# Rounds of the state-space layer in another order, states exchanged by GpSimd, an output product kept whole

## The chip, the cores and the metric

The kernel runs on one core of a Trainium2 chip. The metric is the device time of one execution in microseconds; a kernel is run several times and the median counts. TensorE (PE) multiplies matrices out of SBUF into PSUM, VectorE (DVE) and ScalarE (ACT) work element by element, GpSimd (POOL) does that too and issues transfers, SyncE (SP) only issues transfers. Each engine executes its own queue; they wait for one another through semaphores.

## The reference

A two-layer decoder trunk for one sequence of 1024 tokens and width 1024, all in float32. Layer 0 is a block-diagonal state-space mixer: the normed and modulated input is projected to u and z; u is cut into 64 groups of 16 channels, each with 64 complex states.

```python
u, z = jnp.split(h @ w_in, 2, axis=-1)
bu = einsum('blgc,gpc->blgp', u, bb)            # complex: real and imaginary part
s[l] = abar * s[l-1] + bu[l]                    # associative scan over the tokens
y = einsum(s_r, C_re) - einsum(s_i, C_im) + D * u
y = gelu(y)
y = y * sigmoid(y @ w_glu + b_glu) * silu(z)
x = x + gate * (y @ w_out)
```

Then keys, values and forget gates are computed once from x, and layer 1 is attention with 16 heads whose scores are shifted by the summed forget gates, gated by silu(z) and projected. Every product is computed from float32 operands split into a high and a low part (three products for one), except in the state-space part, which multiplies float32 as it is.

## The kernel before, in words

The text is written against a scheduler: it lists operations in program order, and the scheduler sets the order on each engine from a timeline of its own, restrained where the text says `issue_after`. So what stands on an engine before what is read from the built program.

The change lies in layer 0. The sequence is cut into 128 chunks of 8 tokens. With that, each of the 64 groups becomes four small products: an input matrix (`min`) takes the 8 tokens of 16 channels to the chunk's new state, the states run through a recurrence over the chunks, an output matrix (`moa`) takes the state back to 8 tokens, and the taps (a Toeplitz matrix `minb`) take the tokens of the same chunk to its output. Eight groups make a state block; there are eight blocks, e = 0 to 7, and one round of the main loop per block. In a round stand:

- `products` (DVE, some copies on ACT), twice for half a block: both the input matrix before its turn (`wm`, `tm`) and the output matrix (`moa`), from the powers of the state's factor.
- `turn_in`: TensorE transposes `wm` (`pin`), ACT copies it out into `min`.
- `taps`: TensorE multiplies the output matrix by the input coefficients into `pk`; `toeplitz` then copies `pk` out on ACT into `kev` and SP spreads it by eight transfers into `minb`.
- `states_in`: TensorE multiplies `min` by u into `vps`, ACT copies that out as `v1`; `swap_halves` makes `v2`, the same with the upper and lower 64 partitions (real and imaginary parts) exchanged, by two transfers.
- `tables`: cosines and sines (`cT`, `sT`) by which the states are rotated, so that the recurrence becomes a real one. DVE forms the angles, ACT does Abs and two sines.
- `scan`: DVE rotates the new states (three operations) and runs the recurrence; SP then exchanges the halves of its result, again by `swap_halves`.
- `rotate_back`: three DVE operations, of which the second needs the exchanged result.
- `states_out`: TensorE adds `minb` by u and `moa` by the rotated state into `py`; ACT applies the gelu, for which it loads another table, and then loads the sines' table again; GpSimd stores the result with eight transfers.

The helpers are `tt` and `mul` (line 218), so DVE's operations of all these steps have one line and are told apart by their tiles. `ve` and `te` chain the steps on DVE and on TensorE in the order in which they are written; ACT, POOL and SP are left to the scheduler. Between the steps TensorE works on the projections of u and z: `unit()` takes one half of a chunk (12 matrix products) from `strips`. Their results are copied out of PSUM on ACT (`ut`, `ez`) and stored by SP; the weights are split into a high part on ACT (`w_hi`, line 95) and a low part on DVE (`w_lo`, line 103).

Buffers that matter here: `moa` has two, used in turn by the blocks; `wm`, `min`, `pk`, `kev`, `cT`, `sT` and `dT` have one; `minb` has two, and `v1`, `v2`, `r1` two each. `dT` holds the decay for the recurrence; ACT fills it.

After the rounds come the gate's product, the output product (`pj_o`) and the residual sum. In the output product each strip of 128 channels is done for one half of the tokens at a time, in the order of OUT_SEQ. `mean` sums the squares of the finished half over the channels (two matrix products, `ms`); for the first half it is called between the two halves of the next strip's product, as `between`.

## Time and profile before

| | us |
|---|---|
| median of 3 runs (lowest, highest) | 1168.27 (1167.28, 1170.02) |
| profiled execution | 1168.8 |
| its span, first to last instruction | 1167.0 |
| PE, DVE, ACT, POOL busy | 1139.6, 838.2, 609.1, 350.1 |
| mean granted clock of TensorE | 0.997 |

The projections for the state-space layer begin in the first 20 us; the scans of the eight rounds start between 105.8 and 266.3 us; the gate's product begins at 291.3 us, the output product at 380.6 us, and keys, values, queries and attention fill the rest. Page rows give a line, engine, operation, output<-input and count, then busy time, mean ns and the idle time just before, with what ended it. Timeline rows give start, duration and the instruction, with a wait in brackets. Rows of waits give the sum, the number and the longest. Window rows give a stretch, its length, the busy times of PE, PEld, DVE, ACT and POOL with counts, the granted clock, the DMA share and GB/s.

### The profile page before, as it was taken

Reading aid. Unit: us, or ns where it says so; the run is one execution under the profiler, and the core shown is the slowest. Engines: PE = TensorE matmul, PEld = TensorE weight load, DVE = VectorE, ACT = ScalarE, POOL = GpSimd, SP = SyncE. Lnnn points to the kernel's source line nnn. Section 1 sums busy time; section 2 is a strip of 40 time slices with the busy share of each in tenths; the row PEclk is TensorE's granted clock in tenths of the full one; section 3 lists DMA queues with packets and bytes.
Section 4 is the critical chain, followed back from the end, with each engine's and each line's share of the span. In section 5 each row is a group of like instructions: output and inputs, shape, how many; then the busy total and the mean of one; then the engine's idle time right before and its main releaser. Section 6 shows DMA issues by size and latency. Waiting matters only on the chain.

```text
span 1167.0 us, 20630 instructions
## 1 busy us (share of the span) xinstructions
PE 1139.6 (98%) x7506; PEld 1015.0 (87%) x7506; DVE 838.2 (72%) x1735; ACT 609.1 (52%) x1152; POOL 350.1 (30%) x581
## 2 busy tenths in 40 slices
PE   9999998999999999999999999999999999999998
PEld 7688887888888887999999999988988898887886
DVE  7869998875888875935767754358888888898431
ACT  6565776675535332522232443247777777787210
POOL 2300112113000133211254455435455554544100
PEclk9999999999999999999999999999999999999999
DMA  9664567467975773148844249236556564741151
GB/s 358 219 178 144 145 161 197 128 155 255 323 261 197 262 276 117 73 181 271 294 157 169 109 140 277 91 126 146 113 124 138 117 130 107 155 100 63 53 174 72
DMA packets 95109, 197.11 MB, mean 169 GB/s; under 512 B 17728, under 2 KB 43008, under 8 KB 93472
## 3 DMA queue, kind: packets, MB, share of 16 engines
q1 hardware_dynamic: 86336, 170.76, 48.9%
q0 software_dynamic: 6928, 20.26, 5.4%
q10 hardware_dynamic: 1744, 4.77, 1.7%
q8 instruction: 59, 0.97, 0.4%
q14 instruction: 42, 0.34, 0.1%
HBM read 138.21 MB, written 46.27 MB: 158 GB/s over the span
## 4 chain that ended last, share of the span: by engine, by line
PE 78%; DVE 9%; ACT 6%; DMA 5%; issue 2%; POOL 0%; SPq 0%; ACTq 0%; DVEq 0%
PE tkps L990 23%; PE pj_g L114 8%; PE pj_o L114 8%; PE zb L114 6%; PE u L269 5%; PE pj_f L114 4%; PE tp L1240 4%; PE z L269 3%; PE ov L1246 3%; PE f L114 3%; PE ov L1247 3%; DMA v<-v 2%; PE sp L1207 2%; PE sp L1208 2%; ACT pr L1215 1%
## 5 line engine op out<-in xcount | busy, mean ns | idle before, releaser
L990 PE MATMUL tkps<-wvh,aH 128*128 128x256 f32 (+1 forms) x768 | 218.2, 285 | 1.4 <-DVE hnt L1019 1.4
L990 PE MATMUL tkps<-wvl,aH 128*128 128x256 f32 (+1 forms) x768 | 215.4, 281 | 0.0
L990 PE MATMUL tkps<-wvh,aL 128*128 128x256 f32 (+1 forms) x768 | 214.7, 281 | 0.0
L990 PEld LDWEIGHTS tkps<-wvh,aH 128*128 128x128 f32 x768 | 144.3, 188 | 2.4 <-issue 1.7
L990 PEld LDWEIGHTS tkps<-wvl,aH 128*128 128x128 f32 x768 | 144.6, 188 | 0.4 <-issue 0.2
L990 PEld LDWEIGHTS tkps<-wvh,aL 128*128 128x128 f32 x768 | 144.0, 188 | 0.5 <-issue 0.5
L1217 POOL TENSOR_SCALAR pr<-pr,sm 128x128 f32<-128x128 f32 (+7 forms) x128 | 95.3, 750 | 91.7 <-DVE sm L1216 91.6
L1242 ACT ACTIVATE pth<-tp 128x512 fp32r<-128x512 f32 (+1 forms) x192 | 86.9, 489 | 50.6 <-PE ov L1246 29.5
L1215 ACT ACTIVATE pr<-pr,mx 128x128 f32<-128x128 f32 (+7 forms) x128 | 98.9, 773 | 24.9 <-DVE mx L1212 23.9
L1243 DVE TENSOR_TENSOR ptl<-tp,pth 128x512 fp32r<-128x512 f32 (+1 forms) x192 | 101.0, 551 | 9.7 <-ACT pth L1242 8.6
L95 ACT ACTIVATE w_hi<-w_raw 128x1024 fp32r<-128x1024 f32 x47 | 49.7, 1057 | 79.7 <-PE pj_f L114 20.1
L740 POOL DMA_DIRECT2D y_d<-r x60 | 31.3, 552 | 190.5 <-ACT r L734 189.5
L1212 DVE CUSTOM_DVE_ANT_0 pr<-sp,msk 128x512 f32<-128x512 f32 (+3 forms) x128 | 72.6, 569 | 21.6 <-PE tp L1240 15.5
L1240 PE MATMUL tp<-ident,pr 128*128 128x128 f32 x576 | 82.1, 273 | 2.6 <-DVE ptl L1243 2.6
L1246 PE MATMUL ov<-pth,vhl 128*128 128x256 f32 x320 | 84.0, 295 | 0.2
L1247 PE MATMUL ov<-ptl,vhl 128*128 128x256 f32 x320 | 79.7, 283 | 0.2
L1240 PEld LDWEIGHTS tp<-ident,pr 128*128 128x128 f32 x576 | 68.6, 141 | 12.4 <-DVE ptl L1243 2.1
L1014 ACT ACTIVATE hsq<-tkps 128x256 f32<-128x256 f32 x64 | 24.6, 384 | 104.6 <-PE tkps L990 104.4
L1017 POOL TENSOR_TENSOR hms<-hms,nhalf 128x4 f32<-128x4 f32 x64 | 71.7, 1121 | 5.3
L1207 PE MATMUL sp<-kk,qs 128*128 128x256 f32 (+2 forms) x192 | 69.9, 367 | 0.6 <-DVE mx L1212 0.5
L1019 DVE TENSOR_TENSOR hnt<-tkps,hms 128x256 f32<-128x256 f32 x64 | 27.0, 422 | 53.7 <-POOL hms L1017 53.6
L1208 PE MATMUL sp<-kk,q 66*128 66x256 f32 (+2 forms) x192 | 65.6, 345 | 0.0
(366 smaller groups left out, 3196.3 us busy)
## 6 DMA issues: line engine op xcount, KB each, us to landing
modw<-modw SPq DMA_DIRECT2D x48, 512.0 KB
wvr<-kvq_w SPq DMA_DIRECT2D x12, 1024.0 KB
w_raw<-a_w_in SPq DMA_DIRECT2D x16, 512.0 KB
v_d<-vt POOLq DMA_DIRECT2D x32, 256.0 KB, 4.0
kk<-k_d SPq DMA_DIRECT2D x16, 512.0 KB
vhl<-v_d SPq DMA_DIRECT2D x16, 512.0 KB
qs<-q_d SPq DMA_DIRECT2D x32, 256.0 KB
w_raw<-a_w_out SPq DMA_DIRECT2D x10, 512.0 KB
```

The source lines that it names most:

```text
L114: m = T.matmul(ps, w[wt][:, k, :], act[at][k][half], start=(k == k0 and n == 0), stop=(k == k1 and n == 2)).ins
L269: m = T.matmul(ps[:, 0:c1 - c0], w[wt][:, k, :], act[at][k][i][:, c0:c1], start=(k == 0 and n == 0), stop=(k == KT - 1 and n == 2)).ins
L990: last_tk[:] = [T.matmul(ps[:, 0:nv], at, wt[:, k, 0:nv], start=(n == 0), stop=(n == 3 * KT - 1)).ins]
L1207: T.matmul(sp[:, 0:wm_], qsl, kk[:, 0, lo:lo + wm_], start=True, stop=False)
L1208: sp_end.append(T.matmul(sp[:, 0:wm_], q1_[:, P * i:P * i + P], kk[0:HD + 2, 1, lo:lo + wm_], start=False, stop=True).ins)
L1215: S.activation(pr[:, 0:nk], pr[:, 0:nk], AF.Exp, scale=-1.0, bias=mx, accum_out=sm)
L1217: G.tensor_scalar(out=pr[:, 0:nk], in0=pr[:, 0:nk], scalar1=sm, scalar2=0.0, op0=ALU.mult, op1=ALU.add)
L1240: T.transpose(out=tp[:, b, :], in_=prs[qi][:, P * (b0 + b):P * (b0 + b) + P], identity=ident)
L1242: S.activation(pth[:, 0:m, dst], tp[:, 0:m, :], AF.Copy)
L1243: V.tensor_tensor(out=ptl[:, 0:m, dst], in0=tp[:, 0:m, :], in1=pth[:, 0:m, dst].bitcast(F32), op=ALU.subtract)
L1246: T.matmul(ov, vhl[:, b, :], pth[:, b - b0, :], start=(b == 0), stop=False)
L1247: end = T.matmul(ov, vhl[:, b, :], ptl[:, b - b0, :], start=False, stop=(b == nb - 1)).ins
```

## The change

`products` is cut into `mat_in` (wm, tm) and `mat_out` (moa, dd). In a round, `mat_out` of the next block's second half stands behind `rotate_back`, and on TensorE `states_in` is followed at once by `states_out`, then the second `taps`; the half unit that stood between comes after. The new states are exchanged by GpSimd instead of ACT. `dT` is filled in `tables` instead of in `scan`, behind the copy of the new states. In `mat_out` the product by the imaginary powers goes first. In the output product, the strip that follows `mean` is issued behind the whole of the strip that holds it.

```diff
-        def project(w, act, half, nm, pool=None, tag="pj", between=None):
+        def project(w, act, half, nm, pool=None, tag="pj", between=None, ends=None):
...
                 with tc.issue_after(m):
-                    project_part(ps, w, act, half, range(KT // 2, KT))
+                    ends.append(project_part(ps, w, act, half, range(KT // 2, KT)))
...
-                S.activation(cT, sT, AF.Abs, bias=half)
+                with tc.issue_after(st["ev"]):
+                    S.activation(dT[:, :, 1:], dec[:, n8].unsqueeze(2).broadcast_to([P, 8, NCH - 1]), AF.Copy)
+                    S.activation(cT, sT, AF.Abs, bias=half)
...
+            def mat_in(e, hb, st):
...
+                return tt(w7, w7, tm, ALU.add)
+
+            def mat_out(e, hb, st):
...
+                mul(tm2, x2m[:, gs].unsqueeze(2).broadcast_to(sh), pwi[:, gs].unsqueeze(3).broadcast_to(sh))
                 mul(moa[:, ls, 1:], x1m[:, gs].unsqueeze(2).broadcast_to(sh), pwr[:, gs].unsqueeze(3).broadcast_to(sh))
-                mul(tm2, x2m[:, gs].unsqueeze(2).broadcast_to(sh), pwi[:, gs].unsqueeze(3).broadcast_to(sh))
...
-                    S.activation(v1[:, 4 * hb:4 * hb + 4], vp_, AF.Copy)
-                swap_halves(v2, v1)
+                    st["ev"] = S.activation(v1[:, 4 * hb:4 * hb + 4], vp_, AF.Copy).ins
+                swap_halves(v2, v1, G)
...
-                S.activation(dT[:, :, 1:], dec[:, 8 * e:8 * e + 8].unsqueeze(2).broadcast_to([P, 8, n1]), AF.Copy)
...
-                    ve(products, e + 1, 1, b_)
+                    ve(mat_in, e + 1, 1, b_)
                     te(turn_in, 1, b_)
                     unit()
-                    te(taps, e + 1, 1, b_)
                     te(states_in, e + 1, b_)
                 ve(rotate_back, a_)
                 if more:
+                    ve(mat_out, e + 1, 1, b_)
+                    ve(tables, e + 1, b_)
+                    te(states_out, e, a_, b_["sin"])
+                    te(taps, e + 1, 1, b_)
                     toeplitz(e + 1, b_)
-                    ve(tables, e + 1, b_)
-                unit(1 if more else 6)
+                else:
+                    unit(6)
+                    te(states_out, e, a_, None)
                 if e + 2 < KT:
-                    ve(products, e + 2, 0, c_)
-                te(states_out, e, a_, b_.get("sin"))
+                    ve(mat_in, e + 2, 0, c_)
+                    ve(mat_out, e + 2, 0, c_)
+                if more:
+                    unit()
...
+                with ExitStack() as own:
+                    for m in whole[-1:]:
+                        own.enter_context(tc.issue_after(m))
+                    ps = project(held[e][1], act, i, f"o{e}_{i}", psa, "psa", pending, whole if pending else None)
```

On DVE, in round 4, from the recurrence (L712, now L718) to the third operation of rotate_back. Before:

```order
L712 SCALAR_TENSOR_TENSOR v_2187<-dT,r_2182 128x1024
L103 TENSOR_TENSOR w_lo<-w_raw,w_hi 128x1024
L218 TENSOR_TENSOR wm<-bb,rvr 128x64x7
L218 TENSOR_TENSOR tm<-bbs,rvi 128x448
L218 TENSOR_TENSOR moa<-x1m,pwr 128x4x128
L218 TENSOR_TENSOR wm<-wm,tm 128x64x7
L218 TENSOR_TENSOR tm_2288<-x2m,pwi 128x512
L218 TENSOR_TENSOR moa<-moa,tm_2288 128x4x128
L218 TENSOR_TENSOR r_2182<-cT,v_2187 128x1024
L218 TENSOR_TENSOR sT<-sT,v_2188 128x1024
```

Now:

```order
L718 SCALAR_TENSOR_TENSOR v_2187<-dT,r_2182 128x1024
L103 TENSOR_TENSOR w_lo<-w_raw,w_hi 128x1024
L218 TENSOR_TENSOR wm<-bb,rvr 128x64x7
L218 TENSOR_TENSOR tm<-bbs,rvi 128x448
L218 TENSOR_TENSOR wm<-wm,tm 128x64x7
L218 TENSOR_TENSOR r_2182<-cT,v_2187 128x1024
L218 TENSOR_TENSOR sT<-sT,v_2188 128x1024
L218 TENSOR_TENSOR r_2182<-r_2182,sT 128x1024
L218 TENSOR_TENSOR tm_2327<-x2m,pwi 128x512
L218 TENSOR_TENSOR moa<-x1m,pwr 128x4x128
```

The three operations of the output matrix (moa and its tm) have moved from between the recurrence and rotate_back to behind rotate_back.

On ACT, in round 4, around the copies of the taps (kev), the tables of block 5 (cT and sT) and the gelu of block 4 (r<-py). Before:

```order
L681 ACTIVATE kev<-pk 16x2x128 x4
L697 ACTIVATE v_2317<-vps 128x512 x2
L612 DMA v_2318<-v_2317 64x1024 x2
L625 ACTIVATE cT<-sT,half 128x1024
L626 ACTIVATE cT<-cT,nhpi 128x1024
L627 ACTIVATE sT<-sT,npi,ntpi 128x1024
L734 ACT_TABLE_LOAD
L734 ACTIVATE r_2384<-py 128x512
L645 ACTIVATE moa<-x1m 128x4x16
L734 ACTIVATE r_2384<-py 128x512
L737 ACT_TABLE_LOAD
```

Now:

```order
L423 ACTIVATE ez_2267<-z_2_2268 128x32x8
L704 ACTIVATE v_2307<-vps 128x512
L626 ACTIVATE dT<-dec 128x8x127
L627 ACTIVATE cT<-sT,half 128x1024
L656 ACTIVATE moa<-x1m 128x4x16 x2
L628 ACTIVATE cT<-cT,nhpi 128x1024
L629 ACTIVATE sT<-sT,npi,ntpi 128x1024
L740 ACT_TABLE_LOAD
L740 ACTIVATE r_2339<-py 128x512 x2
L743 ACT_TABLE_LOAD
L688 ACTIVATE kev<-pk 16x2x128 x4
```

The copies of the taps have moved from ahead of the new states to behind the gelu and the table load after it. So it is in rounds 0, 4 and 6; in rounds 1, 2 and 3 they stand ahead of Abs (L627), in round 5 behind it and ahead of the two sines.

On SP, from the last transfers of block 5's taps (minb) to its exchange of states (L612). Before:

```order
L684 DMA minb_956<-kev 16x8x48
L684 DMA minb_956<-kev 16x8x32
L684 DMA minb_956<-kev 16x8x16
L688 DMA uu<-u_d 128x8x128
L426 DMA z_d<-ez_2266 128x512
L612 DMA v_2421<-v_2420 64x1024 x2
```

Now:

```order
L691 DMA minb_956<-kev 16x8x48
L691 DMA minb_956<-kev 16x8x32
L691 DMA minb_956<-kev 16x8x16
L612 DMA v_2421<-v_2420 64x1024 x2
L426 DMA z_d<-ez_2266 128x512
L426 DMA z_d<-ez_2267 128x512
```

The eight transfers of the taps stand ahead of the exchange in both; the load of u and the store of z no longer stand between.

More of the change, by code (lines that the diff above doesn't have):

```diff
@@ L795, in trunk @@
             toeplitz(0, sts[0])
-            ve(products, 1, 0, sts[1])
+            ve(mat_in, 1, 0, sts[1])
+            ve(mat_out, 1, 0, sts[1])
             unit(2)
@@ L905, in trunk @@
             gate_a = mod_bias(16, 24, "gate_a")
+            whole = []
             held, acc, seen, pending = {}, [None] * 2, [0, 0], None
```

31 lines of the change are left out of this document (16 added, 15 removed).

## The prediction

> **What bounds the kernel now.** I read the page first, then the windows, the waits, and the timelines of single engines.
>
> ```profile
> PE 1139.6 (98%) x7506; PEld 1015.0 (87%) x7506; DVE 838.2 (72%) x1735; ACT 609.1 (52%) x1152; POOL 350.1 (30%) x581
> ```
>
> TensorE is busy for 98% of the span, so no edit can gain much: all its idle time together is 27 us. But the change lies in one stage, the rounds over the eight state blocks, and that stage has a limit of its own. I take the stretch from the first to the last multiply of rotate_back that needs the turned-over state (sT by v, in L218).
>
> ```profile
> 114.64:275.30 160.66, 151.13 (x1127) 135.29 (x1126) 138.63 (x171) 110.26 (x165) 32.46 (x62) 0.99 0.62 156
> ```
>
> The columns are the stretch, its length, then busy time of PE, PEld, DVE, ACT, POOL. Seven rounds take 160.66 us, 23.0 each. PE is busy for 151.1 of it, DVE for 138.6. Both are close to full, and the chain runs through both: rotate_back on DVE releases the output products (py) on PE, and their end releases a DVE write. The waits of DVE in this stretch:
>
> ```profile
> DVE moa L218 <- PE py L731: 6.0, 3, 2.6
> DVE sT L218 <- DMA v<-v: 5.3, 3, 4.4
> DVE r L218 <- ACT cT L626: 3.7, 1, 3.7
> DVE w_lo L103 <- ACT w_hi L95: 2.9, 3, 2.1
> DVE v L218 <- DMA v<-v: 1.0, 1, 1.0
> DVE bi L403 <- PE u L269: 0.9, 1, 0.9
> ```
>
> With 0.2 us for a bias copy these are 20.0 of the 22.0 us that DVE is idle; 2.0 us are gaps too small for a row. So the stage is a DVE chain: 138.6 of work, 2.0 of gaps, 20.0 of waits. No DVE operation is added or dropped, so I recount the waits alone.
>
> **What goes.** The output matrix (moa) of round e+2 is written into the buffer that py of round e reads. It now comes after tables, and py no longer stands behind half a projection unit on PE. The durations, from the round at 208 us of DVE and of PE:
>
> ```profile
> 208.27 1.22 DVE L218 TENSOR_TENSOR sT<-xhi,ylo 128x1024 f32<-128x1024 f32 x1
> ...
> 210.67 0.18 DVE L218 TENSOR_TENSOR dd<-dsk,idg 128x32 f32<-128x32 f32 x1
> ...
> 212.62 0.69 DVE L218 TENSOR_TENSOR tm<-x2m,pwi 128x512 f32<-128x512 f32 x1
> ```
>
> ```profile
> 212.11 0.39 PE L730 MATMUL py<-uu,minb 128*128 128x128 f32 x2
> ...
> 215.46 0.39 PE L731 MATMUL py<-r,moa 128*128 128x128 f32 x2
> ```
>
> By the starts tables takes 2.4 us and mat_in with dd 1.95; mat_out takes 1.94 (next part). From the end of rotate_back, DVE does one mat_out, tables and mat_in before it writes moa again, 6.3 us, against 3.7 us for py. The 6.0 us go. The waits on w_hi and the bias copy (4.0) will lie within the swap waits below.
>
> **The swap loses its cover.** After the scan, SP exchanges the halves of the state and rotate_back must wait for it. One round of the DVE timeline:
>
> ```profile
> 220.85 2.29 DVE L712 TENSOR_TENSOR_SCAN v<-dT,r 128x1024 f32<-128x1024 f32 x1
> 223.69 1.23 DVE L103 TENSOR_TENSOR w_lo<-w_raw,w_hi 128x1024 fp32r<-128x1024 f32 x1 [0.54 <-ACT w_hi L95]
> 224.83 0.62 DVE L218 TENSOR_TENSOR wm<-bb,rvr 128x448 f32<-128x448 f32 x1
> ...
> 227.22 0.69 DVE L218 TENSOR_TENSOR tm<-x2m,pwi 128x512 f32<-128x512 f32 x1
> ...
> 228.56 1.22 DVE L218 TENSOR_TENSOR r<-cT,v 128x1024 f32<-128x1024 f32 x1
> 229.69 1.22 DVE L218 TENSOR_TENSOR sT<-sT,v 128x1024 f32<-128x1024 f32 x1
> ```
>
> From w_lo to the multiply by sT it is 6.0 us. Of this the moa operations (1.94: 0.60 between the rows shown, the rest from 227.22 to 228.56) move behind rotate_back; the cover falls to 4.05 us. How long the swap takes is seen from DVE's multiplies, of which two waited, and SP's issues:
>
> ```profile
> 173.96 2.29 DVE L712 TENSOR_TENSOR_SCAN v<-dT,r 128x1024 f32<-128x1024 f32 x1
> ...
> 183.15 1.23 DVE L218 TENSOR_TENSOR sT<-sT,v 128x1024 f32<-128x1024 f32 x1 [0.64 <-DMA v<-v]
> ...
> 275.30 1.23 DVE L218 TENSOR_TENSOR sT<-sT,v 128x1024 f32<-128x1024 f32 x1 [4.43 <-DMA v<-v]
> ```
>
> ```profile
> 177.49 0.32 SPq L426 DMA_DIRECT2D z_d<-ez  x1
> 177.91 1.15 SPq L612 DMA_DIRECT2D v<-v  x2
> ...
> 268.58 1.15 SPq L612 DMA_DIRECT2D v<-v  x2
> ```
>
> That is 5.2 and 6.7 us here, and rounds that did not wait under a cover of 6.0 had less than that. I take 5.7. The upper bound is 6.7. The lower is 4.1: the GpSimd row below for 256 KB (3.5) and half a microsecond for the second half's issue. So an undisturbed round now waits 1.65 us. This is rounds 2 and 4: 3.3 us.
>
> **SP's queue.** The first rows of both views also show that SP issues in its written order: the scan of that round ended at 173.96 + 2.29 = 176.25, and its swap went out at 177.91, behind a z_d store that waited for its data. In the changed order two things stand ahead of the swap. In rounds 3 and 6 it is such a z_d store again; its copy on ACT comes after both table loads, so that the swap is 1.8 us late and DVE waits 3.4: 6.8 us.
>
> The second is larger. In each round eight minb transfers stand on SP ahead of the next swap, and they read kev, which ACT copies out of the taps. Taps is now last on PE, and in rounds 0, 4 and 6 of the changed order kev stands on ACT behind the sines, the gelu and the table load that follows it. ACT's rows of the round at 211 us, and SP's minb:
>
> ```profile
> 207.64 1.53 ACT L681 ACTIVATE kev<-pk 16x256 f32<-16x256 f32 x4
> ...
> 211.49 1.15 ACT L625 ACTIVATE cT<-sT,half 128x1024 f32<-128x1024 f32 x1 [1.20 <-DVE sT L483]
> ...
> 217.51 1.28 ACT L737 ACT_TABLE_LOAD   x1
> ```
>
> ```profile
> 209.20 6.70 SPq L684 DMA_DIRECT2D minb<-kev  x8
> ```
>
> Let W be the time at which DVE's tables are done. From Abs to the end of the second table load ACT needs 217.51 + 1.28 - 211.49 = 7.3 us, then kev 1.53: W + 8.9. Eight issues take 6.7 us here; while ACT issues no swap beside them I expect fewer, and the last three take 1.90 together:
>
> ```profile
> 214.01 1.90 SPq L684 DMA_DIRECT2D minb<-kev  x3
> ```
>
> So 5.2 is the lower bound and my choice, 6.7 the upper: SP is free at W + 14.1. DVE ends the next scan at W + 9.9 (mat_in 1.8, dd 0.1, mat_out 1.9, scan 5.9, gaps). The swap leaves 4.2 us late. Now the cover: in round 1 it is 5.2 us, as three small projection operations stand in it, so the wait is 4.7; in round 5, 4.2 + 5.7 - 4.05 = 5.85. For round 7 there is no second table load and no mat_in: kev at W + 7.6, minb until 12.8, scan end at 8.3, 4.5 late, and the cover is w_lo and one multiply, 2.3: the wait is 7.9. Together 18.45 us. In the kernel before, kev was over 2 us ahead of Abs, and none of this was seen.
>
> **Tables later on ACT.** Where kev stands ahead of Abs or the sines (rounds 1, 2, 3, 5), it delays them by its 1.53 us. DVE has 3.9 us of matrices between; I count 1.5, 0, 0.6 and 0.5 us by the copies that stand with it. The last round keeps a wait of 2.3 for the cosine, without matrices to cover it. Sum 4.9.
>
> **Exchange of new states by GpSimd.** ACT no longer issues two transfers per round, 1.12 us:
>
> ```profile
> 210.32 1.12 ACTq L612 DMA_DIRECT2D v<-v  x2
> ```
>
> ACT is not full (110.3 of 160.7), so this only moves Abs a little; I count nothing. GpSimd is idle then. Its own issues, size and median time to landing:
>
> ```profile
> x_d<-x POOLq DMA_DIRECT2D x16, 256.0 KB, 3.5
> yl<-y_d POOLq DMA_DIRECT2D x7, 512.0 KB, 11.8
> ```
>
> At the size of the first row, landing is some 5 us after the eviction, which ends about with rotate_back. The multiply that reads it comes 9.3 us after that (mat_out, tables, mat_in, mat_out, one multiply). The cover is tables, matrices and the first multiply of the scan; without it, each microsecond would count in each round. The Trainium skill's page "DMA: Bandwidth & Descriptors" (Issuing engines are not separate DMA queues) says that another issuing engine saves only the sequencer's time; by it the move is worth 1.1 us of ACT per round at most, and 0 if ACT is not waited for. No row contradicts it. For scan 0 the new state comes earlier:
>
> ```profile
> 102.74 1.22 DVE L218 TENSOR_TENSOR v<-sT,v 128x1016 f32<-128x1016 f32 x1 [1.02 <-DMA v<-v]
> ```
>
> I take 0.8 us off, the sine bounding the rest.
>
> **PE's clock.** PE now waits about 5 us for the last rotate_back. After one long wait PE's timeline and the window behind it show this:
>
> ```profile
> 203.41 0.68 PE L659 MATMUL pin<-ident,wm 128*128 128x128 f32 x4 [3.24 <-DVE wm L218]
> ```
>
> ```profile
> 203.80:206.60 2.80, 2.80 (x15) 2.57 (x12) 2.77 (x4) 0.81 (x2) 0.00 (x0) 0.51 0.35 135
> ```
>
> The granted clock is 0.51 for 2.8 us, a loss of 1.4. In earlier rounds the slow matmuls lie under DVE's chain; after the last one PE bounds again, and over the longer py (3.7) I take 1.7. The Trainium skill's page "TensorE: Matmul & The Clock Gate" (Part 1) gives half rate after an idle window of about 3.4 us and as long to recover, half of which would be the same 1.7; the trace agrees.
>
> **Output product kept whole.** The second matmul of the mean needs sq and now directly follows the first:
>
> ```profile
> 450.18 1.02 PE L934 MATMUL ms<-sq,onesm 128*128 128x512 f32 x2
> ```
>
> ```profile
> 450.77 0.63 ACT L923 ACTIVATE sq<-x 128x512 f32<-128x512 f32 x1 [6.73 <-DVE x L919]
> ```
>
> sq is ready at 451.4, which costs about 0.4 us. The whole products free their weights in turn, which removes this wait:
>
> ```profile
> 462.05 0.50 PE L114 MATMUL pj_o<-aH,w_hi 128*128 128x512 f32 x1 [1.15 <-ACT w_hi L95]
> ```
>
> Net 0.75 off.
>
> **Sum.** The stretch: 138.63 + 2.0 + 3.3 + 6.8 + 18.45 + 4.9 = 174.1, 13.4 more than 160.66. With -0.8, +1.7, -0.75 that is +13.55. The profiled execution took 1168.8 us (span 1167.0), 0.5 above the median of 1168.27; against the median 1181.8 us.
>
> **Rivals.** (A) The queue holds nothing back, because kev and minb finish before the scan. For it: eight minb finished early in each round so far. Against it: they would have to go out within 1.0 us. Then the 18.45 become 0.5 + 1.65 + 3.4 = 5.55 and the sum is +0.65: 1169 us. (B) As A, and the swap also lands in its lower bound of 4.1: rounds 2 and 4 wait 0.1, 3 and 6 together 3.6, 1, 5 and 7 1.9; the sum is 10.05 less than A, -9.4: 1159 us, faster. The stretch would be 151.1, just PE's own busy time. It decides from a swap under about 5 us without a late issue. For it speak the GpSimd rows and 6.0 us of waits that surely go; against it the 6.7. (C) GpSimd's transfer lands late, as the seven yl loads on its queue do (median 11.8 us): 1.1 + 11.8 - 9.3 = 3.6 us in each of seven rounds, 25 us, 1207. Against it: the rows of its size. That nothing moves is excluded by the order.
>
> **Chances.** Forecast 0.66, own range 1175 to 1190 (minb at 6.7 adds 4.5, a swap at 6.7 up to 7; ACT's waits gone take 5); A 0.09; B 0.20; C 0.05. About 0.2% (2.3 us) is what can be told from no change. Faster 0.20, same 0.09, slower 0.71. To leave 2 in 10 out, the range must reach through A to B's upper part: 1163 to 1190.
>
> **What would show it.** Right: DVE waits of 5 us and more at sT by v in rounds 1, 5 and 7, minb issues on SP just ahead of the swap and after a table load, no wait of moa on py, PE waiting at py, clock halves after it. Wrong: swaps issued at the scan's end in all rounds (A), sT waits under 1 us (B), or DVE waiting at v for the GpSimd transfer (C).

## The result, and the profile after

The changed kernel takes 1196.82 us (median of 5 runs, 1195.32 to 1198.92), the kernel before, run beside it, 1167.58 us (1165.42 to 1170.02). The ratio is 1.0249, with an interval of 1.023 to 1.0269: slower, by about twice what was forecast, and above the end of the range. The profiled execution took 1195.72 us, with a span of 1193.9 and a mean granted clock of 0.987. The medians differ by 29.2 us, the spans of the two profiled executions by 26.9 (1193.9 less 1167.0); the pieces below account for the latter.

From the page of the kernel after, its busy times:

```profile
PE 1150.4 (96%) x7506; PEld 1025.5 (86%) x7506; DVE 836.9 (70%) x1735; ACT 608.0 (51%) x1152; POOL 357.1 (30%) x597
```

No engine got more instructions to do, but for GpSimd's 16 issues. PE is busy for 11 us more, with the same 7506 matmuls, at a mean granted clock of 0.987 instead of 0.997. The rest of the 26.9 us is waiting. Three windows of the kernel after show where: the stretch of the prediction, from the first to the last multiply by sT; the piece from there to the first matmul of the gate's product; and the slow part inside that piece. The columns are as in the prediction (busy time of PE, PEld, DVE, ACT, POOL, the granted clock, the DMA share, GB/s).

```profile
114.20:301.60 187.40, 162.51 (x1140) 145.73 (x1138) 140.20 (x173) 111.22 (x169) 40.52 (x77) 0.95 0.58 151
301.60:319.60 18.00, 15.48 (x89) 14.40 (x90) 8.34 (x11) 8.48 (x14) 2.12 (x4) 0.81 0.43 141
302.20:309.00 6.80, 4.88 (x23) 4.88 (x24) 3.06 (x3) 1.65 (x2) 0.00 (x0) 0.50 0.55 193
```

The same second piece in the kernel before:

```profile
275.30:291.20 15.90, 14.55 (x102) 13.28 (x101) 8.26 (x11) 8.98 (x15) 2.66 (x5) 1.00 0.91 348
```

The remaining bounds are the first matmuls of the gate's product, in the rows of its tile, whose start stands behind the mean times, and of the stage behind the output product (tkps), which starts at 472.8 us before and at 500.3 after. The gate's product, first in the kernel before, then in the one after:

```profile
L114 PE MATMUL pj_g<-aH,w_hi x128: 388/395/399, 291.2 to 379.8; 128*128 128x512 f32 x128
```

```profile
L114 PE MATMUL pj_g<-aH,w_hi x128: 388/395/399, 319.6 to 408.1; 128*128 128x512 f32 x128
```

| piece | before | after | difference | forecast |
|---|---|---|---|---|
| to the first multiply by sT | 114.64 | 114.2 | -0.4 | -0.8 |
| first to last multiply by sT | 160.66 | 187.40 | +26.7 | +13.4 |
| from there to the gate's product | 15.9 | 18.0 | +2.1 | +1.7 |
| gate's product to tkps | 181.6 | 180.7 | -0.9 | -0.75 |
| the rest | 394.2 | 393.6 | -0.6 | 0 |

So the whole of the miss against the forecast, 13.3 us, lies in the stretch. The longest waits of DVE in it, kernel after (the first row counts 1.04 us that end just as the stretch begins):

```profile
DVE sT L218 <- DMA v<-v: 27.6, 7, 14.7
DVE w_lo L103 <- ACT w_hi L95: 6.6, 4, 2.8
DVE biz L421 <- PE z L269: 4.2, 3, 1.9
DVE et L383 <- PE u L269: 4.1, 1, 4.1
```

All of them but one lie between a scan and the multiply by sT that follows it; the exception is a wait of biz of 1.94 us in round 4. Such a segment is made of two parts: how late after the scan the swap is issued, and how long from the issue until the multiply starts. SP's issues show the first part, here of rounds 1, 2, 4 and 7, with the transfers that stood ahead in rounds 1 and 7:

```profile
130.47 5.14 SPq L691 DMA_DIRECT2D minb<-kev  x8
135.71 1.18 SPq L612 DMA_DIRECT2D v<-v  x2
...
158.86 1.15 SPq L612 DMA_DIRECT2D v<-v  x2
...
208.30 1.26 SPq L612 DMA_DIRECT2D v<-v  x2
...
283.52 6.40 SPq L691 DMA_DIRECT2D minb<-kev  x8
290.01 1.25 SPq L612 DMA_DIRECT2D v<-v  x2
```

And DVE's timeline the second, for the same four rounds, with the scans of rounds 4 and 7:

```profile
139.90 0.69 DVE L383 TENSOR_TENSOR et<-u,q2x 128x512 f32<-128x512 f32 x1 [4.12 <-PE u L269]
140.66 1.23 DVE L218 TENSOR_TENSOR sT<-sT,v 128x1024 f32<-128x1024 f32 x1
...
165.21 1.23 DVE L218 TENSOR_TENSOR sT<-sT,v 128x1024 f32<-128x1024 f32 x1 [2.39 <-DMA v<-v]
...
205.56 2.29 DVE L718 TENSOR_TENSOR_SCAN v<-dT,r 128x1024 f32<-128x1024 f32 x1
216.71 1.23 DVE L218 TENSOR_TENSOR sT<-sT,v 128x1024 f32<-128x1024 f32 x1 [2.71 <-DMA v<-v]
...
282.22 2.29 DVE L718 TENSOR_TENSOR_SCAN v<-dT,r 128x1024 f32<-128x1024 f32 x1
301.58 1.23 DVE L218 TENSOR_TENSOR sT<-sT,v 128x1024 f32<-128x1024 f32 x1 [14.69 <-DMA v<-v]
```

In round 7 the scan ends at 282.22 + 2.29 = 284.51, the swap is issued at 290.01, 5.50 late, and 11.57 us later the multiply starts. In round 4 the swap is only 0.45 late, but takes 8.41. Over the seven rounds:

| round | 1 | 2 | 3 | 4 | 5 | 6 | 7 | sum |
|---|---|---|---|---|---|---|---|---|
| issued late by | 4.39 | 0.03 | 0.44 | 0.45 | 5.32 | 1.76 | 5.50 | 17.9 |
| forecast | 4.2 | 0 | 1.8 | 0 | 4.2 | 1.8 | 4.5 | 16.5 |
| issue to multiply | 4.95 | 6.35 | 6.25 | 8.41 | 4.84 | 7.31 | 11.57 | 49.7 |
| forecast | 5.7 | 5.7 | 5.7 | 5.7 | 5.7 | 5.7 | 5.7 | 39.9 |

The lateness came near to what was worked out; the landing did not. In round 1 the time from issue to multiply is only an upper bound of the landing, since the multiply did not wait for the swap: the first row shows that DVE waited for u, from PE. PE had waited for kev, which ACT copies behind the gelu:

```profile
130.46 0.42 PE L678 MATMUL pk<-moa,bb 128*32 128x128 f32 x8 [3.21 <-ACT kev L688]
```

So the late kev holds this round back by two ways at once, through SP's queue and through PE.

The landing is short in rounds 1 and 5, in which the swap was held back. What else was moving suggests a reason. GpSimd's issues in the kernel after:

```profile
127.85 4.21 POOL L746 DMA_DIRECT2D y_d<-r  x8 [6.36 <-ACT r L740]
...
156.70 4.21 POOL L746 DMA_DIRECT2D y_d<-r  x8 [10.53 <-ACT r L740]
...
205.71 4.20 POOL L746 DMA_DIRECT2D y_d<-r  x8 [15.22 <-ACT r L740]
...
282.37 4.20 POOL L746 DMA_DIRECT2D y_d<-r  x8 [7.67 <-ACT r L740]
286.50 3.81 POOL L858 DMA_DIRECT2D yl<-y_d  x7
```

The eight stores of the gelu's result (y_d) set off 2.2 to 3.9 us ahead of the swap in rounds 2, 3, 4 and 6: 158.86 - 156.70 = 2.2 in round 2, 2.6 in round 4. In round 1, the late swap came 7.9 us behind them. These stores stood near the swap in the kernel before too; there they set off 2.9 to 5.4 us ahead of the scan's end, now 2.1 to 3.6. Round 2 of the kernel before, whose scan ended at 154.29:

```profile
150.97 4.16 POOL L740 DMA_DIRECT2D y_d<-r  x8 [18.43 <-ACT r L734]
```

So the change moved them closer, by one to three microseconds in most rounds, and no more than that. The experiments test whether these transfers are the cause. In round 7 the seven loads of 512 KB (yl), which read those stores, set off 3.5 us ahead of the swap; in the kernel before they went out behind it.

### The profile page after: what moved, and what is told of

It is laid out like the page before. It is cut to its first block, busy times and chain, and to the rows that moved or that the text cites. A ratio compares the mean times of both kernels' runs of the same rounds, so it can differ in the third digit from the quotient of the medians.

```text
span 1193.9 us, 20649 instructions
## 1 busy us (share of the span) xinstructions
PE 1150.4 (96%) x7506; PEld 1025.5 (86%) x7506; DVE 836.9 (70%) x1735; ACT 608.0 (51%) x1152; POOL 357.1 (30%) x597
## 4 chain that ended last, share of the span: by engine, by line
PE 75%; ACT 8%; DVE 8%; DMA 5%; issue 2%; SPq 1%; POOL 0%; ACTq 0%; DVEq 0%
PE tkps L1009 23%; PE pj_g L114 7%; PE pj_o L114 7%; PE u L269 6%; PE zb L114 6%; PE pj_f L114 4%; DMA v<-v 4%; PE tp L1259 4%; PE ov L1265 2%; PE f L114 2%; PE ov L1266 2%; PE sp L1226 2%; PE sp L1227 2%; ACT pr L1234 1%; PE z L269 1%
## 5 line engine op out<-in xcount | busy, mean ns | idle before, releaser
L95 ACT ACTIVATE w_hi<-w_raw 128x1024 fp32r<-128x1024 f32 x47 | 49.7, 1057 | 87.2 <-PE pj_f L114 20.1
L269 PE MATMUL z<-aH,w_hi 128*128 128x258 f32 (+2 forms) x192 | 65.6, 342 | 5.6 <-ACT ez L423 5.6
L269 PE MATMUL z<-aL,w_hi 128*128 128x258 f32 (+2 forms) x192 | 64.0, 333 | 0.0
```

Source lines behind the costliest of these rows:

```text
L269: m = T.matmul(ps[:, 0:c1 - c0], w[wt][:, k, :], act[at][k][i][:, c0:c1], start=(k == 0 and n == 0), stop=(k == KT - 1 and n == 2)).ins
```

## The experiments

Two theories divide the loss in the stretch. Q: the lateness, that is, the eight transfers of the taps on SP that wait for kev behind the gelu. L: the landing, that is, other transfers under way. Each experiment is an edit of the kernel after or, where said, of the one before; times are medians, and a ratio is against the kernel before.

### The transfers of the taps issued by GpSimd

```diff
-                    Q.dma_start(out=mi[j:P:8, :, j:8, :], in_=kev[:, :, 0:8 - j, :])
+                    G.dma_start(out=mi[j:P:8, :, j:8, :], in_=kev[:, :, 0:8 - j, :])
```

> The changed kernel with one edit: the eight minb transfers of each round are issued by GpSimd, so that nothing that reads kev stands ahead of the swap on SP. Theory Q (the queue): in the changed kernel the swap left 4.4, 5.3 and 5.5 us after the end of the scan in rounds 1, 5 and 7, and the last one landed 11.6 us after its issue because the seven yl loads went out just ahead of it. All four go: 4.4 + 5.3 + 5.5 + 4.9 = 20 us less, 1177 (1174 to 1184, since part of it shows up as waits on PE's projections). Rival W (the waits on w_hi and on the bias copies, 15 us, and the lost cover set the end, whoever issues minb): at most 5 us less, 1192 or more.

1195.69 us, ratio 1.0245 (1.023 to 1.0261): no gain. The swaps did go out early (0.02 to 1.25 us after the scan), but from issue to multiply it was 6.7 to 10.2 us, and a new wait came. The waits of PE between 95 and 325 us in this kernel:

```profile
PE py L736 <- DMA minb<-kev: 13.4, 3, 12.1
```

The last output product waited 12.1 us for the taps' transfers, which now stood on GpSimd among the yl loads. The edit replaced one queue by another and does not separate Q from L.

### The yl loads behind the last swap

```diff
-                with tc.issue_after(stored[KT if k == KT - 1 else KT - 2]):
-                    last_y = (Q if k == KT - 1 else G).dma_start(out=yls[k], in_=y_rows(k)).ins
+                with tc.issue_after(stored[KT if k == KT - 1 else KT - 2]), tc.issue_after(swapped[0]):
+                    last_y = Q.dma_start(out=yls[k], in_=y_rows(k)).ins
```

> The changed kernel with one edit: all yl loads are issued by SP behind the last swap, not by GpSimd ahead of it. minb stays where it is. Theory Q: the last swap lands in about 6.7 us instead of 11.6, the wait of the last sT multiply falls from 14.7 to about 10, and the time by 5 us to 1192 (1190 to 1194). Rival: the last swap is slow for another reason (its own late issue, or transfers other than yl), then 1197 as in the changed kernel, or more, since the yl loads are later.

1189.58 us, ratio 1.0188 (1.0171 to 1.0205), 7.2 us less than the kernel after. The last swap and the multiply that reads it, on SP and on DVE:

```profile
289.68 1.18 SPq L612 DMA_DIRECT2D v<-v  x2
```

```profile
294.94 1.23 DVE L218 TENSOR_TENSOR sT<-sT,v 128x1024 f32<-128x1024 f32 x1 [7.93 <-DMA v<-v]
```

The swap is issued as late as before, and lands in 5.26 us instead of 11.57. This is L, in one round, by itself: of the 11.57 us, these loads cost 6.3.

### The taps ahead of the tables

```diff
                     ve(mat_out, e + 1, 1, b_)
-                    ve(tables, e + 1, b_)
-                    te(states_out, e, a_, b_["sin"])
                     te(taps, e + 1, 1, b_)
                     toeplitz(e + 1, b_)
+                    ve(tables, e + 1, b_)
+                    te(states_out, e, a_, b_["sin"])
```

> The changed kernel with one edit: taps of a round and the copies of kev stand ahead of the output products again, everything else stays, so that kev on ACT stands ahead of the sines and of the gelu in every round. Theory Q: minb is out before the scan ends, the swap leaves at the end of the scan in rounds 1, 5 and 7, and ahead of the yl loads in the last round: 20 us less, of which kev ahead of the cosine in rounds 0, 4 and 6 takes 4.5 back: 1181 (1178 to 1186). Rival W: at most 5 us less, 1192 or more.

1182.65 us (1178.91 to 1190.57), ratio 1.0139 (1.0095 to 1.0184): 14 us less, as expected, though its four runs lie 11.7 us apart. The stretch of the fastest, which was profiled, is 171.96 us. The price is a wait of PE for the output matrix, in the same kernel:

```profile
PE pk L678 <- DVE moa L218: 13.8, 7, 4.1
```

Taps last is thus the costliest of the parts that were tried one by one, with about half of the loss. The lateness falls from 17.9 to 2.5 us and the last swap, now issued ahead of the yl loads, lands in 6.34 us, so both Q and L change and this run doesn't part them.

### The exchange of new states by ACT again

```diff
-                swap_halves(v2, v1, G)
+                swap_halves(v2, v1, S)
```

> The changed kernel with one edit: the exchange of new states is issued by ACT again, not by GpSimd; no other instruction moves but a bias copy. My prediction counted the move to GpSimd as 0 in the rounds and -0.8 us in the first scan: so here 1197.5, within 1196 to 1200. Rival C (GpSimd's transfer is late and is waited for): faster than the changed kernel by several us, 1190 or less. Rival D (the 1.1 us of issue on ACT stands on the path to the cosine in each round): 8 us slower, 1205.

1193.9 us, ratio 1.0227 (1.0212 to 1.0242): 2.9 us less, where 0.7 more was expected. In its profile 2.0 of it lie in the stretch (185.4) and 0.9 ahead of it. The move to GpSimd, which I had counted at -0.8, costs. How, this run doesn't tell.

### The taps' copies ahead of the gelu on ACT

The gelu is written behind taps and made to wait for kev; PE's order stays.

```diff
                     te(taps, e + 1, 1, b_)
                     toeplitz(e + 1, b_)
+                    with tc.issue_after(b_["sin"]):
+                        outputs(e, a_, b_["kev"])
```

> The changed kernel with one edit: on ACT the gelu of a round, with its two table loads, waits behind the copies of kev; the order on TensorE is the same to a matmul. Theory Q: kev is 3.65 us earlier (1.09 for two gelus and 2.56 for two loads) in rounds 0, 4 and 6, so minb is out earlier, the swap leaves 3.7 us earlier in rounds 1, 5 and 7, the last one ahead of the yl loads (5 us more), and taps no longer waits for kev's buffer: 11 + 5 = 16 us less, 1181 (1177 to 1186). Rival W (the waits on w_hi and bias copies fill the time): at most 5 us less, 1192 or more.

1185.64 us, ratio 1.016 (1.0142 to 1.0177): 11.2 us less, of 16 expected. SP in round 7 of this kernel:

```profile
281.05 5.35 SPq L691 DMA_DIRECT2D minb<-kev  x8
286.49 1.19 SPq L612 DMA_DIRECT2D v<-v  x2
```

The swap goes out 2.07 us after the scan instead of 5.50, and over all rounds the lateness falls from 17.9 to 6.2 us, so the queue is what made the swaps late. But the landings are 5.76, 9.11, 7.02, 8.65, 8.28, 7.10 and 6.02, 51.9 us together, more than the 49.7 of the kernel after. In rounds 1 and 5 the swap now goes out 2.8 and 2.6 us behind the stores of y_d, not 7.9 and 8.9, and takes 0.8 and 3.4 us longer to the multiply. In rounds 1 to 6 together the swaps go out 8.3 us earlier and take 7.8 us longer, so the freed queue gains 0.5 us there. The gain lies in round 7, 9.0 us from the scan to the multiply: 3.4 of lateness, and 5.55 because the yl loads now set off behind the swap, which lands in 6.02.

### The swap ahead of the stores

On the kernel of the last experiment: GpSimd issues the swap after the scan, and the stores of the gelu's result wait until that is issued.

```diff
-                swapped[:] = [swap_halves(r3, r2, Q)]
+                swapped[:] = [swap_halves(r3, r2, G)]
...
+                    with tc.issue_after(swapped[0]):
+                        stored[e] = q.dma_start(out=y_d[e, :, i, :].rearrange("(c g) k -> c g k", c=GC), in_=yb[GC * i:GC * i + GC]).ins
...
                 ve(scan, e, a_)
+                if e:
+                    store(e - 1, sts[e - 1])
```

> As e4_kev_before_gelu, and the swap after the scan is issued by GpSimd, ahead of the eight y_d stores of the round before, which wait behind it on GpSimd's queue; the last one also stands ahead of the yl loads there. Theory S (the swap is slow to land because the y_d stores share the DMA engines with it, and still late behind SP's z_d): in e4 it took 6.5 to 9.2 us from the end of the scan to the multiply by sT in rounds 1 to 6 and 8.1 in round 7; without the stores about 5.3 as in round 0. The sum of the differences is 21 us, of which TensorE's own work allows no more than 15 to 18: 1169 (1167 to 1175). Rival: other transfers (minb, weights, z_d) slow it, and only the late issue goes, 6 us: 1179 or more.

1173.2 us, ratio 1.005 (1.0035 to 1.0065), 23.6 us less than the kernel after. Its stretch and the piece behind it:

```profile
115.55:276.50 160.95, 146.65 (x1087) 131.30 (x1086) 139.69 (x172) 108.57 (x164) 43.34 (x83) 0.99 0.57 147
276.50:295.40 18.90, 18.90 (x135) 17.57 (x134) 6.82 (x9) 8.60 (x14) 6.48 (x13) 1.00 0.98 347
```

GpSimd's issues and DVE's multiplies of rounds 2 and 7 in this kernel:

```profile
157.40 1.01 POOL L612 DMA_DIRECT2D v<-v  x2 [14.91 <-DVE v L718]
158.41 3.70 POOL L757 DMA_DIRECT2D y_d<-r  x7
...
271.89 1.02 POOL L612 DMA_DIRECT2D v<-v  x2 [8.74 <-DVE v L718]
```

```profile
163.78 1.23 DVE L218 TENSOR_TENSOR sT<-sT,v 128x1024 f32<-128x1024 f32 x1 [2.68 <-DMA v<-v]
...
276.50 1.22 DVE L218 TENSOR_TENSOR sT<-sT,v 128x1024 f32<-128x1024 f32 x1 [2.50 <-DMA v<-v]
```

Every swap goes out 0.3 us after its scan. Issue to multiply is 5.89, 6.38, 4.84, 5.77, 6.09, 5.94 and 4.61, 39.5 us in all: seven times 5.64. (In rounds 3 and 4 the multiply did not wait for the swap.) That is the forecast's 5.7. The stretch is back at the length that it had before the change (160.95, 160.66). The span is 4.2 us above that before; 3.0 of this stand in the second row: PE did 40 matmuls fewer in the stretch than before (1087, 1127) and does most of them behind it, fully busy. So L and Q together are the loss of the stretch. The issuing engine, the place of kev and the order of the stores changed together here. For the yl loads the order is shown by itself, by the run above in which they stand behind the last swap. For the stores it is argued only: in the kernel after, where SP issued all swaps, 4.84 us (8.9 behind the stores) stands beside 8.41 (2.6 behind them), but the run before this one has 5.76 and 6.02 beside 8.28, all three 2.6 to 2.8 us behind the stores.

### The last kernel, with the output matrix ahead of rotate_back

```diff
-                ve(rotate_back, a_)
                 if more:
                     ve(mat_out, e + 1, 1, b_)
+                ve(rotate_back, a_)
+                if more:
                     ve(tables, e + 1, b_)
```

> As e8_swap_ahead_of_stores, and the second half of the output matrix stands between the scan and rotate_back again (1.94 us of VectorE's work under the swap in rounds 1 to 6). Theory V (VectorE's chain sets the rounds): with a swap of 5.3 and a cover of 6.0 the waits on it vanish in rounds 1 to 6; 1.3 us each, 8 us less than e8. Theory P (TensorE's idle time sets them): its waits for rotate_back grow shorter by the same 1.3 us in the rounds where it waits there and nothing is won in the others: 2 to 5 us less than e8.

1179.71 us, ratio 1.0099 (1.0083 to 1.0115), 6.5 us more, against both expectations. DVE's waits between 115 and 290 us in this kernel:

```profile
DVE w_lo L103 <- ACT w_hi L95: 15.2, 5, 5.5
```

The weights arrive late: ACT's w_hi waited 9.8 us for their load, and DVE behind it. Why they are late in this order wasn't settled. The swap stands ahead of the stores here too, but in round 1, where the multiply waited for it, it took 7.87 us, not 5.89: being ahead of the stores does not by itself make the landing short.

### More work for PE in its waits

Matmuls into a spare tile that nothing reads, 11, 6 and 24 of them, fill PE's waits in round 6, in the last round and ahead of the last output product; in another run, 48 fill the last of these alone.

```diff
+                if not more:
+                    te(fill, 6)
...
+                    if e == 6:
+                        te(fill, 11)
...
+                    te(fill, 24)
```

> The changed kernel with added work: matmuls of the identity into a spare PSUM buffer where TensorE waits late in the rounds: 11 in round 6 ahead of the z product that waits 3.3 us for a copy, 6 in round 7, and 24 ahead of the last output product, which waits 5.7 us. Theory C (the half clock after a wait is on the path): the half-rate stretch after the last output product (6.8 us, 3.4 us lost) goes, and the one in round 6 (1.7 us lost): 1192 (1190.5 to 1194). Rival: the halved clock lies under other waits, the same 1197; if the added matmuls get in the way, more.

1195.82 us, ratio 1.0243 (1.0227 to 1.0259): no gain. From 257 us to the scan's end of round 7, first the kernel after, then this one:

```profile
257.00:285.10 28.10, 22.57 (x159) 20.90 (x158) 20.61 (x21) 18.26 (x26) 8.00 (x16) 0.94 0.46 114
```

```profile
257.00:285.00 28.00, 25.51 (x191) 23.32 (x191) 20.91 (x22) 17.05 (x25) 9.12 (x18) 1.00 0.49 118
```

The clock is held at 1.00 and nothing is won: in rounds 6 and 7 the slow matmuls lie under DVE's chain, as forecast. Round 1 was not filled; there the granted clock was 0.52 from 131.40 to 134.80 in the kernel after, behind the wait for kev, while PE worked on the products u, for the last of which DVE then waited. The 24 did not prevent the slow piece after the last wait. The 48 did:

```diff
+                    te(fill, 48)
                     te(states_out, e, a_, None)
```

> The changed kernel with 48 added matmuls of the identity into a spare PSUM buffer ahead of the last output product, about 5.3 us of TensorE's 5.7 us of waiting there. Theory C (the half clock after this wait is on the path): the half-rate stretch of 6.8 us behind it goes, 3.4 us less than the changed kernel: 1193.4 (1192.5 to 1195). Rival: the stretch stays or its loss is covered by the store and load of y behind the last output product: 1196.8 within 1.

```profile
303.30:319.20 15.90, 15.90 (x116) 14.81 (x115) 9.73 (x13) 9.76 (x16) 2.13 (x4) 1.00 0.50 158
```

The piece from the last multiply by sT to the gate's product is 15.9 us again, not 18.0: the clock cost 2.1 us there. The whole run took 1195.9 us all the same, ratio 1.0245 (1.0231 to 1.0259): its stretch is 189.17 us, 1.8 more, with a last swap that landed in 13.39 us.

### The kernel before, with the output product kept whole

Of the change, only the last two pieces of the diff (`ends`, `whole`).

> The kernel before with the output product behind the mean kept whole, and nothing else of the change. The prediction gave -0.75 us for this part: 1166.7. In the changed kernel the stretch from the gate products to the first key products is 0.8 us shorter than before, so the same -0.8 is expected by the trace; a rival in which the part costs time (the mean's second matmul waits for sq) gives 1168 or more.

1166.3 us, median of 12 runs, ratio 0.9985 (0.9975 to 0.9995): 1.0 us less, by an interval that just leaves out 1. No kernel here is faster than this one.

### The same, with a third buffer for the output matrix

```diff
-                    st["moa"] = sbm.tile([P, 8, 9, GC], F32, name="moa", tag="moa")
+                    st["moa"] = sbm.tile([P, 8, 9, GC], F32, name="moa", tag="moa", bufs=3)
```

> The kernel before with the output product kept whole and a third buffer for moa, so that VectorE writes the output matrix of round e+2 without waiting for py of round e (6.0 us of waits in three rounds), in the old order. Theory V (the rounds are a VectorE chain, as the prediction had it): 6 us less, 1161. Theory P (TensorE's own idle time and clock bound the rounds: 8.4 us of waits of it in this stretch, none of which is on moa): no more than 2 us less, 1165 to 1167.

1166.42 us, 12 runs, ratio 0.9988 (0.9976 to 0.9999): nothing gained. Without the third buffer DVE waits 6.0 us for py before it writes moa, as in the kernel before. With it, this wait is absent from DVE's waits in the stretch, and these rows stand there:

```profile
DVE r L218 <- ACT cT L626: 4.7, 2, 4.3
DVE w_lo L103 <- ACT w_hi L95: 4.1, 2, 2.1
DVE v L218 <- DMA v<-v: 3.4, 3, 2.3
```

The stretch is as long (160.34 us without, 160.37 with), and DVE is idle for 22.3 us of it (21.8 without). These three waits together are 4.5 us longer than without the third buffer.

### The old order, with the exchange by GpSimd and the product whole

```diff
-                swap_halves(v2, v1)
+                swap_halves(v2, v1, G)
```

> The changed kernel with the old order of the rounds: the kernel before, the exchange of new states by GpSimd, the output product kept whole. If the order of the rounds is the whole loss, as the places of the waits say, this is as fast as the kernel before with the output product kept whole: 1166.3, within 1165 to 1168.5 (in the new order the exchange by GpSimd cost up to 2.9 us). If GpSimd's exchange is waited for by itself, 1170 or more.

1170.77 us, ratio 1.0029 (1.0019 to 1.0038): 4.5 us more than the kernel with the whole product alone. GpSimd, SP and DVE at the last swap:

```profile
266.14 3.95 POOL L843 DMA_DIRECT2D yl<-y_d  x7
```

```profile
266.42 1.16 SPq L612 DMA_DIRECT2D v<-v  x2
```

```profile
276.12 1.23 DVE L218 TENSOR_TENSOR sT<-sT,v 128x1024 f32<-128x1024 f32 x1 [7.42 <-DMA v<-v]
```

The rounds run faster, if anything: the swap is issued at 266.42, against 268.37 with the whole product alone. But the yl loads now set off just ahead of it, and it lands in 9.70 us; there they set off 1.4 us behind it, and it landed in 6.31. Behind the longer wait, PE's clock halves too (18.4 us from the last multiply by sT to the gate's product). This is where the exchange by GpSimd costs, in this order.

In the next two kernels GpSimd issues the last swap ahead of the yl loads.

```diff
-                swapped[:] = [swap_halves(r3, r2, Q)]
+                swapped[:] = [swap_halves(r3, r2, G if e == KT - 1 else Q)]
...
-                with tc.issue_after(stored[KT if k == KT - 1 else KT - 2]):
+                with tc.issue_after(stored[KT if k == KT - 1 else KT - 2]), tc.issue_after(swapped[0]):
```

> As e10_old_order, and the swap of the last round alone is issued by GpSimd, in its queue ahead of the seven yl loads. Theory Y (in e10 the exchange by GpSimd makes the rounds 1.5 us shorter up to the last scan, and the loss is the last swap, which left 0.3 us after the first yl load and took 9.7 us instead of 6.3): the last swap lands in 4.6 to 5.3 us as in e8 and e2, so the last multiply by sT is 4 us earlier than in e10, TensorE waits under 1 us at the last output product and its clock is not halved there (3.4 us): 7 us less than e10, 1164 (1162.5 to 1165.5), faster than both kernels. Rival: yl, now 1 to 2 us later, is waited for by the gate product; then what is won is lost again, 1166.3 or more.

1170.24 us, ratio 1.0023 (1.0013 to 1.0033). The edit moved a split of weights on DVE (w_lo) as well, which then waited 5.08 us. With that held in its place:

```diff
-            with tc.issue_after(swapped[0]):
+            with tc.issue_after(swapped[0]), tc.issue_after(order[0]):
```

> As e11_last_swap_ahead, with the split of the gate weights on VectorE behind the last rotate_back, where it stands in e10_old_order: against e10 only the queue of the last swap differs. Theory Y (the cost of GpSimd's exchange in e10 is the collision of the last swap with the yl loads): the last multiply by sT comes 5 us after the swap's issue instead of 9.7, TensorE waits 0 to 1 us at the last output product, no half clock after it (3.4 us in e10): 1164 (1162.5 to 1166), below the kernel before. Rival: the loss of e10 lies elsewhere (a later arrival of the yl loads or of the gate weights is waited for): 1168 or more.

1168.92 us, ratio 1.0014 (1.0004 to 1.0023). The swap lands in 7.38 us instead of 9.70. PE still waits 2.92 us for the last rotate_back, its clock still halves, and the last piece is 18.5 us:

```profile
273.20:291.70 18.50, 15.94 (x89) 14.86 (x90) 8.96 (x12) 8.43 (x15) 2.14 (x4) 0.82 0.73 269
```

The expectation was 1164. The swap ahead of the yl loads gives back 1.9 of the 4.5 us, and it still takes 7.38 with the loads 1.1 us behind it. The last piece is 2.7 us longer than with the whole product alone (18.5, 15.8): PE idles 1.3 us more in it, and is busy 1.4 us longer on fewer matmuls, at the lower clock. That this is where the 2.6 us left come from is argued from the pieces, not tried.

## Why the prediction was right and wrong

- **The stretch as a chain of DVE: right for the most part.** DVE's busy time is 140.20 us (138.63 before), so nearly all of the growth is its waits. PE's clock in rounds 6 and 7 costs nothing, as the filled kernel shows. But the chain is not DVE's alone: in round 1 it runs through PE.
- **SP's queue: right.** The sum of the lateness was put at 16.5 us and came to 17.9; rounds 1, 5 and 7 are the late ones, by the mechanism named, and kev ahead of the gelu takes most of it away. In round 3 the z_d store no longer stood in the way (0.44 instead of 1.8). The sign named for it, waits of 5 us and more at sT by v in rounds 1, 5 and 7, came in round 7 alone (14.69): round 1 shows no such wait and round 5 one of 2.56, since the waits for u and for w_hi stand ahead of the multiply in the same segments.
- **The swap's landing: wrong; this is the step that failed.** "I take 5.7", with 6.7 as the upper bound, treated the landing as a property of the swap. From issue to multiply it was 49.7 us over the seven rounds instead of 39.9: 9.8 of the 13.3 us missed. Of these, 5.9 are round 7, where the yl loads had set off ahead of the swap and it took 11.57; with the loads behind it, 5.26. The other 3.9 are rounds 2, 3, 4 and 6 (6.25 to 8.41), less what rounds 1 and 5 came out below 5.7. With all swaps ahead of stores and loads the mean is 5.64 again. That the stores of y_d make the difference in rounds 2 to 6 is not shown: they had set off 2.9 to 5.4 us ahead of the scan's end before as well. The remark that each transfer of a moved step counts was followed for the queues, and not for what is in flight; the yl loads, whose median of 11.8 I had quoted, entered only as rival C.
- **The 5.7 was also read too low.** The prediction speaks of two multiplies that waited, but its row of waits counts three. The third is in round 1; on SP and on DVE of the kernel before:

```profile
132.62 1.15 SPq L612 DMA_DIRECT2D v<-v  x2
```

```profile
139.26 1.23 DVE L218 TENSOR_TENSOR sT<-sT,v 128x1024 f32<-128x1024 f32 x1 [0.28 <-DMA v<-v]
```

That is 6.64 us, beside 5.24 and 6.72: a mean of 6.2, by which the sum would be 3.5 us higher. The rounds that did not wait bound the landing only by 5.80, 5.87, 6.51 and 7.97 us, not all by 6.0.

- **The rest of the stretch's miss.** Of the other 3.5 us, 1.4 are the lateness (17.9 less 16.5). The other 2.1 lie between the multiply by sT and the next scan's end. "No DVE operation is added or dropped" holds for the kernel, but not for the stretch: the output matrix of round 0 stood ahead of the first multiply by sT, and stands behind it now, inside the stretch. So 13 sets of moa and its tm lie in it instead of 12, and DVE's busy time is 1.6 us longer. The waits nearly cancel: those for the tables (cT), put at 4.9, came to 2.8, and a bias copy (1.94) and a copy that waited for kev (0.84) came in.
- **"The 6.0 us go": the wait went, the time did not.** The kernel with a third buffer removes this wait from the old order and gains nothing. A wait in a chain with little slack may be counted off only where the next limit lies that far away; here other waits and gaps took over.
- **The waits on w_hi and the bias copies within the swap waits: right in the sum.** They show, with the wait for u in round 1, as 14.9 us of waits of their own, of which 13.0 lie in the segments from scan to multiply.
- **The exchange by GpSimd: wrong in sign.** Put at 0 in the rounds and -0.8 for scan 0; measured as +2.9 in the new order and +4.5 in the old. No wait of DVE on this transfer stands among the rows of the stretch, so rival C was rightly given little. In the old order it moves the yl loads ahead of the last swap, which explains part of it; in the new one the cause is open.
- **PE's clock: right in size.** 1.7 was forecast for the last piece, 2.1 measured. In the rounds nothing was forecast; that holds for rounds 6 and 7, and is open for round 1. The Trainium skill's page "TensorE: Matmul & The Clock Gate" (Part 1), on which an estimate of 1.7 rested, gives about 3.4 us for the recovery; here the clock was at 0.50 for 6.8 us, and matmuls ran in 4.88 of them.
- **The whole product: right.** -0.75 was forecast; the piece gained 0.9 and the kernel with it alone 1.0.
- **Rivals.** A needed punctual swaps that land as before. The run with the swap ahead of the stores brings both about (0.3 us late, 5.64), and its stretch, 160.95, is what A's sum gives (174.1 less 12.9, or 161.2). B needed a landing of 4.1 as well, which no measured swap reached (the shortest took 4.40), so B's stretch of 151.1 was never tried; its 0.20 rested on a landing that the rows of the kernel before, 5.24 at the least, spoke against.

## What to carry to other kernels

When a change moves the moment at which an exchange on the critical path is issued, list what else will be in flight then, not only what stands ahead of it in its queue; a duration read from the trace holds only beside the transfers that it had there, and all the rows that show it should be read. A wait that is removed counts as a gain only if the next limit of the chain is known; a spare buffer is a cheap run that tells. And a change of many parts is worth splitting: one part of this one gained 1.0 us, and the others together lost 30.

## What the runs showed of the hardware

- **The landing of a transfer depends on what else is in flight.** The same two transfers of 256 KB within the chip's memory (the swap), where DVE waited for them, took 9.7 to 13.4 us behind seven loads of 512 KB each, and 5.3 to 6.7 where these loads set off 1.3 us or more behind them. With the first of the loads 0.8 and 1.1 us behind, 10.2 and 7.4 were measured. Some 2 to 5 us behind eight stores of 64 KB each they took 5.2 to 9.1, and 1.0 us ahead of such stores 4.6 to 6.4 in one kernel, but 7.9 once in another. What decides within 5.2 to 9.1 is open. The Trainium skill's page "DMA: Bandwidth & Descriptors" (Issuing engines are not separate DMA queues) says that transfers run on the same DMA engines and interleave whichever engine issued them. The runs agree: in the kernel after, the swap was issued by SP and the loads by GpSimd, and it took 11.57 all the same.
- **The clock halves after less waiting than the forecast's example of 3.24 us.** Two successive windows of 3.41 us from the kernel after:

```profile
230.62:234.03 3.41, 1.80 (x21) 1.37 (x20) 2.76 (x2) 3.34 (x8) 3.41 (x7) 0.99 0.63 111
234.03:237.44 3.41, 3.41 (x19) 3.41 (x18) 1.26 (x2) 1.69 (x3) 0.03 (x1) 0.51 0.43 112
```

PE was idle for 1.6 us of the first, in a wait for kev, and the second ran at 0.51. In the kernel before, a window with even less work (1.65 of 3.41 from 224.33) was followed by one at 1.00. Where the bound lies, and on what besides the busy time it depends, is open.
